# The chunk solve on off-diagonal 64x64 tiles, alternating with the next A K^T

## The chip, the cores and the metric

The kernel runs on one core of one Trainium2 chip. The metric is the device time of one execution in microseconds (us): 1723.08, the median of three runs from 1722.53 to 1729.99. Beside it stands one execution taken with the hardware profiler, 1721.11 us, whose traced span is 1719.3 us.

The engines go by the profile's names: PE is TensorE (PEld its weight load), DVE is VectorE, ACT is ScalarE, POOL is GpSimd, and SP is SyncE, which issues the DMAs. Every engine takes its own instructions in order.

## The reference

A two-layer encoder is applied to two groups of 512 tokens (width 1024, 16 heads of 64) with shared weights. Layer 0 is an RWKV-7 time mixing run forward and backward, layer 1 a neighbourhood attention on an 8 x 64 grid; a norm stands before and behind each. The part that matters here is the recurrence of layer 0, for each head and each direction:

```python
def step(s, inp):
    r_t, w_t, k_t, v_t, a_t, b_t = inp
    sa = jnp.einsum('bhvk,bhk->bhv', s, a_t)
    s = s * w_t[:, :, None, :] + sa[..., None] * b_t[:, :, None, :] + v_t[..., None] * k_t[:, :, None, :]
    return s, jnp.einsum('bhvk,bhk->bhv', s, r_t)
```

The kernel does it by chunks of 64 tokens. Within a chunk, the rows U that the term `sa` contributes solve a triangular system, whose right side Z takes the state before the chunk and a masked product A K^T times V. The inverse of the triangular matrix is made ahead. The norm that also plays a part is `x * rsqrt(mean(x*x) + eps) * g`.

## The kernel before

**Stages.** A prelude normalises both groups and does the first projections. `scan_phase` follows: the chunked recurrence of both groups, with the rest of the projections (`flow`) filling PE. `rest` does the attention and the output projections.

**The scan.** The work is a list of 8 items (group s, four heads pb), each with 8 chunks: 64 steps (`Step`, q = 0 to 63). A step holds both directions d, both pairs of heads g, and both heads h of a pair; on the 128 partitions lie two halves of 64. `e = [i % 2, 1 - i % 2]` says which half of the partitions the direction d uses in chunk i. In one step PE does, in this order:

- L1093, only if a chunk went before: the state times the chunk's factors, into the place `zy`, 32 records (a matmul in fp32 is two records in the trace).
- L1099: masked A K^T times V, added in `zy`, 16 records. ACT copies the result as Z (L1105).
- L1119, the solve: U = M Z, 8 matmuls with 64 rows, 64 columns and 64 moving columns, into `us`. Input and output lie in the same half (`r`), so they sit on the diagonal tiles of the 128x128 array, and d, the innermost loop, changes from the one to the other.
- `factors(q + 1)`: the next step's A K^T (L1010, 8 such matmuls on the diagonal tiles, into `room`, the free half of the first bank of this step's `zy`), and its 16 factor matmuls (L1022, into `pf`). If the next chunk isn't there yet, the thread `alone` does them later.
- L1133 and L1137: ACT has copied U into X (L1125), whose other half of the partitions is V, loaded by DMA in `fetch_x`. Tm times X gives the state's update, R times X the output.

DVE masks A K^T (L1045, `near`) and the factors (L1055, `outer`), and updates the state (L1145, L1146).

**What sets the order.** In the scan a planner writes the instructions of PE, DVE and ACT down in a fixed order. Each part of the work is a generator (`Thread`) that yields the engine it wants next, a gate, and the time at which its inputs are there. `weave` keeps a model of the engines' times (`Clock`) and picks the thread that is ready with the lowest rank: steps 0, `near` 0.5, `outer` 1, the norm of the first group 1.2, products (L747 to L749) 9. For PE the model has this rule, in `Clock.matmul`:

```python
for (r, q), x in self.tiles.items():
    if r == tp[0] or q != tp[1]:
        t = max(t, x)
self.tiles[tp] = t + c
self.t["P"] = t + (13.0 if f32 and not tr else 6.5)
```

So it lets a matmul begin beside another one only if that one has the same column half and other rows. `bank(tag)` returns a gate (is a place of this PSUM pool free in the model?) and a time (from when); most PE parts of the scan yield both.

**The norm.** `rstds` (L425) reduces the sum of squares with four matmuls of one column (L430), takes the root, and spreads the result with four matmuls (L442); each of the two takes a place in the pool `pm`. In the scan it runs twice, as part of the thread `norm0(0)`, and yields "P" without a gate. In `rest`, `norm0(1)` is put down together with the output projection of the first group: after each yield that projection goes on by 64/17 of its yields.

Of the kernel before, what the change touches and what calls it, by code (L numbers as in the profile page):

```python
# [2 lines left out]

# [1 line left out]

# [13 lines left out]
P = 128  # L19
# [5 lines left out]
L = 64  # L25
# [24 lines left out]
class Clock:  # L50
# [39 lines left out]
    def room(self, key, bufs):  # L90
        s = self.slots.get(key, ())
        return 0.0 if len(s) < bufs else min(self.left(n) for n in s)
# [121 lines left out]
class Trunk:  # L214
# [69 lines left out]
    def t(self, tag, shape=(P, T), bufs=1, dt=F32, pool=None):  # L284
        x = (pool or self.main).tile(list(shape), dt, tag=tag, bufs=bufs, name=self.name(tag))
        self.clock.new(x.tensor.name, (tag, id(pool or self.main)), bufs)
        return x
# [137 lines left out]
    def rstds(self, acc):  # L425

        nc = self.nc
        ps = self.p("pm", (P, 4))
        for c in range(4):
            nc.tensor.matmul(ps[:, c:c + 1], acc[:, c * P:(c + 1) * P], self.ones[:, 0:1], start=True, stop=True)  # L430
        yield "A"
        r = self.t("rs", (P, 4), 2)
        nc.scalar.activation(r, ps, AF.Sqrt, bias=self.eps[:, 0:1], scale=1.0 / D)
        yield "D"
        nc.vector.reciprocal(r, r)
        dg = self.tmp()
        for c in range(4):
            nc.vector.tensor_scalar(dg[:, c * P:(c + 1) * P], self.ident, r[:, c:c + 1], None, op0=ALU.mult)
        yield "P"
        out = self.p("pm")  # L440
        for c in range(4):
            nc.tensor.matmul(out[:, c * P:(c + 1) * P], self.ones, dg[:, c * P:(c + 1) * P], start=True, stop=True)  # L442
        yield "A"
        nc.scalar.copy(acc, out)
# [545 lines left out]
    def fetch_x(self, st):  # L990
        sp, s, pb, i, e = self.sp, st.s, st.pb, st.i, st.e
        half = lambda h: slice(64 * h, 64 * h + 64)

        st.X = self.t("X", (P, 2, 2, 2, HD), self.NX, F32, self.front)
        for d in range(2):
            self.load(
                st.X[half(1 - e[d]), d].rearrange("t h g c -> t h (g c)"),
                sp["vt", s][pb, i % 2, i // 2, :, :, d].rearrange("h t g c -> t h (g c)"))

    def factors(self, q):  # L1000


        nc, st = self.nc, self.steps[q]
        half = lambda h: slice(64 * h, 64 * h + 64)
        ab, e = st.ab, st.e
        st.ak = self.steps[q - 1].room if q else self.p("pm", (P, 2, 2, L))
        for g in range(2):
            for dd in range(2):
                for h in range(2):
                    nc.tensor.matmul(  # L1010
                        st.ak[half(h), dd, g], ab[half(h), dd, g, 1 + e[dd]], ab[half(h), dd, g, 2 - e[dd]], start=not q, stop=True,
                        skip_group_check=True)
        st.f = self.p("pf", (P, 2, T)).rearrange("p h (x d g t) -> p h x d g t", x=2, d=2, g=2)
        for d in range(2):
            for g in range(2):
                for a in range(2):
                    for h in range(2):
                        rt = ab[half(h), d, g, 3 - 3 * e[d]]

                        both = bass.AP(  # L1020
                            tensor=rt.tensor, offset=rt.offset, ap=[list(rt.ap[0]), [(16 - 8 * d - 4 * g - 3 + 3 * e[d]) * L, 2], [1, L]])
                        end = nc.tensor.matmul(  # L1022
                            st.f[half(a), h, 0, d, g] if st.last else st.f[half(a), h, :, d, g], ab[half(h), d, g, 2 * e[d] + a],
                            rt if st.last else both, start=True, stop=True)
        st.ends = [end]
        self.clock.keep.add(st.f.tensor.name)
        self.did["factors"] += 1
# [12 lines left out]
    def near(self, q):  # L1040

        nc, did, st = self.nc, self.did, self.steps[q]
        yield "D", lambda: did["factors"] > q, lambda c: c.at([st.ak.tensor.name])
        st.AK = self.t("AK", (P, 2, 2, L), self.NAK, F32, self.front)
        nc.vector.tensor_tensor(st.AK, st.ak, self.mstrict.unsqueeze(1).unsqueeze(1).broadcast_to([P, 2, 2, L]), op=ALU.mult)  # L1045
        did["AK"] += 1
# [20 lines left out]
    def step(self, q):  # L1067

        nc, did, st = self.nc, self.did, self.steps[q]
        vt, act = nc.vector, nc.scalar  # L1070
        t = lambda tag, shape, n: self.t(tag, shape, n, F32, self.front)
        half = lambda h: slice(64 * h, 64 * h + 64)
# [4 lines left out]
        free, room = self.bank("zy")  # L1077
# [6 lines left out]
        ab, e = st.ab, st.e  # L1084
# [3 lines left out]
        if st.i:  # L1088
            for d in range(2):
                for g in range(2):  # L1090
                    for a in range(2):
                        for h in range(2):
                            nc.tensor.matmul(  # L1093
                                zy[half(a), h, (a + e[d]) % 2, g], ab[half(h), d, g, 2 - 2 * e[d] + a], before.S[half(h), d, g],
                                start=(d == g == 0), stop=False, skip_group_check=True)
        for g in range(2):
            for d in range(2):
                for h in range(2):
                    nc.tensor.matmul(  # L1099
                        zy[half(e[d]), h, 0, g], st.AK[half(h), d, g], st.V[half(h), d, g],  # L1100
                        start=(st.i == g == 0), stop=True, skip_group_check=True)
        did["states"] += 1
        yield "A"
        Z = t("Z", (P, 2, 2, HD), self.NZ)
# [3 lines left out]
        go = lambda: q + 1 < len(self.steps) and did["factors"] == q + 1 and did["fetch"] > q + 1 and near()  # L1108
# [3 lines left out]
        mt = self.formed[key][1].rearrange("p (h i g) a t -> p h i g (a t)", h=2, i=NCH)  # L1112
        us = self.p("us", (P, 2, 4, HD))
        u = us[:, 0].rearrange("p (h g) v -> p h g v", h=2)
        for g in range(2):
            for h in range(2):
                for d in range(2):
                    r = half(e[d])
                    nc.tensor.matmul(u[r, h, g], mt[r, h, st.i, g], Z[r, h, g], start=True, stop=True)  # L1119
        did["solve"] += 1  # L1120
        if go():
            self.factors(q + 1)
        yield "A", lambda: did["X"] > q
        for d in range(2):
            act.copy(st.X[half(e[d]), d], u[half(e[d])])  # L1125
        yield (
            "P", lambda: did["R"] > q and did["X"] > q,
            lambda c: c.at(name(st.X, st.R[0], *([] if st.last else st.Tm[:1]))) - self.NEAR)
# [5 lines left out]
        for g, h in gh:  # L1134
            for d in range(2):
                r = half(1 - e[d])
# [418 lines left out]
    def scan_phase(self, mid):  # L1555
# [57 lines left out]
        def each(f):  # L1613
# [4 lines left out]
            Thread(lambda: 0, each(self.step)), Thread(lambda: 0.5, each(self.alone)), Thread(lambda: 0.5, each(self.near)),  # L1618
            Thread(lambda: 1, each(self.outer)),
            Thread(lambda: 0, fetch()), Thread(lambda: 0, fetch_x()), *self.flow(), Thread(lambda: 5, inverse()), Thread(lambda: 1.5, preps()),  # L1620
            Thread(lambda: 1.3 if did["finish"] == 3 else 4, finish()), Thread(lambda: 1.2, self.norm0(0))]
        e = mybir.EngineType
# [4 lines left out]
    def run(self):  # L1627
        self.todo = [(s, pb) for s in range(2) for pb in range(4)]
        self.made, self.hid, self.shift = set(), {}, {}
        self.did = Counter()  # L1630
        self.xz, self.os = [], [[], []]
        mid, prep, first = ExitStack(), ExitStack(), ExitStack()
        self.banks(mid, pf=1, pm=5 - self.SG - self.ZY, us=1)
        if self.SG:
            self.banks(mid, pg=self.SG)
        self.zs = ExitStack()
        self.banks(self.zs, zy=self.ZY)
        self.gt = "zy"
        self.lp = self.pool(first, "right")
        a = self.prelude(0)  # L1640
        for _ in range(self.FIRST):
            next(a)
        a = both(a, self.prelude(1))
        run(self.columns(0, "z", self.xz), (a, 1))
        run(self.columns(0, "k", self.shifted(0, 1)), (a, 1))
        run(a)
        self.xr = self.shifted(0, 0)
        first.close()
        self.front = self.pool(mid, "right")
        self.pp = self.pool(prep, "right")  # L1650
        self.AHEAD, self.AHEADW = self.SCAN_A, self.SCAN_W
        self.scan_phase(mid)
        self.rest(prep, mid)
# [58 lines left out]
def both(*gs):  # L1712
    for g in gs:
        yield from g
# [110 lines left out]
```

## Time and profile before

| What | us |
|---|---|
| median of three runs | 1723.08 |
| the profiled execution | 1721.11 |
| its span in the trace | 1719.3 |
| ahead of the scan | 0 to 280 |
| the scan, first A K^T to last chunk | 280 to 1149 |
| attention and output projections | 1149 to 1719 |

All times of the trace are microseconds from the start of the span. The span is 1.8 us shorter than the execution's own time. A row of the groups reads: line, engine, operation, output <- inputs, tile and shape, number of records, then busy time, mean length of one in ns, and the idle time of the engine before them with its releasers. The busy time of a group counts moments in which any of its records runs. The records of matmuls overlap (their ends are modelled), so the distance from one start to the next tells what one costs. A row of the table by stage gives, for each engine, the busy time and the number of its instructions, then the granted clock of PE as a share of full speed, the share of DMA and its GB/s. A row of the waits reads: who waited for whom, the sum in us, how often, the longest.

### The profile page before, as it was taken

What the parts mean: (1) busy time and instruction counts of PE and PEld (TensorE: products, weight loads), DVE (VectorE), ACT (ScalarE), POOL (GpSimd) and SP (SyncE); (2) the same over time, 40 slices, a digit from 0 to 9 for tenths busy, and PEclk for the clock granted to TensorE, in tenths of its full rate; (3) what the DMA queues carried; (4) which work ended last, traced back from release to release, by engine and by line L of the source; (5) the groups of instructions that cost most, each with busy time, mean ns of one, the idle gap of its engine ahead of it and who ended that gap; (6) DMA issues with size and microseconds to landing.
All of it is one profiled execution on the core that took longest, in us unless ns stands there. A gap on an engine that the chain in (4) does not pass through costs nothing. (4 is left out here: it accounts for less than half of the span.)

```text
span 1719.3 us, 45887 instructions
## 1 busy us (share of the span) xinstructions
PE 1583.5 (92%) x18624; PEld 1209.3 (70%) x18624; DVE 1246.5 (73%) x2725; ACT 982.9 (57%) x1975; POOL 24.1 (1%) x94
## 2 busy tenths in 40 slices
PE   7999787999988999789988799999999999999998
PEld 6766555776766767567766677777777787777776
DVE  8986678788877867898788898655565586555474
ACT  5444655767755675656576545544556664555462
POOL 0000000000000000000000000000000000000000
PEclk9989999999999989899999799999999999999999
DMA  5435687786566678766587564547564248555553
GB/s 204 166 117 202 208 278 230 221 273 224 184 201 205 206 239 252 240 217 216 188 263 229 191 209 146 177 147 246 178 197 146 93 147 268 163 164 160 163 169 98
DMA packets 240819, 336.23 MB, mean 196 GB/s; under 512 B 53696, under 2 KB 119360, under 8 KB 240608
## 3 DMA queue, kind: packets, MB, share of 16 engines
q1 hardware_dynamic: 240608, 333.31, 60.4%
q8 instruction: 146, 2.39, 0.6%
q14 instruction: 65, 0.53, 0.1%
HBM read 227.71 MB, written 105.51 MB: 194 GB/s over the span
## 5 line engine op out<-in xcount | busy, mean ns | idle before, releaser
L747 PE MATMUL pm<-act,whi 128*128 128x512 f32 x608 | 272.9, 449 | 13.1 <-ACT whi L699 9.9
L749 PE MATMUL pm<-act,wlo 128*128 128x512 f32 x608 | 248.8, 409 | 18.2 <-DVE wlo L701 18.2
L748 PE MATMUL pm<-act,whi 128*128 128x512 f32 x608 | 248.9, 409 | 7.7 <-DVE act L727 6.1
L404 PE MATMUL pg<-act,whi 128*128 128x512 f32 x448 | 181.4, 406 | 0.0
L405 PE MATMUL pg<-act,whi 128*128 128x512 f32 x448 | 178.1, 398 | 0.0
L406 PE MATMUL pg<-act,wlo 128*128 128x512 f32 x448 | 178.0, 398 | 0.0
L353 ACT CAST whi<-raw 128x512 fp32r<-128x512 f32 x156 | 96.2, 617 | 142.6 <-PE pg L405 71.8
L354 DVE TENSOR_TENSOR wlo<-raw,whi 128x512 fp32r<-128x512 f32 x156 | 106.7, 686 | 73.9 <-ACT whi L353 56.9
L747 PEld LDWEIGHTS pm<-act,whi 128*128 128x128 f32 x608 | 119.3, 196 | 56.3 <-issue 13.9
L749 PEld LDWEIGHTS pm<-act,wlo 128*128 128x128 f32 x608 | 119.9, 197 | 52.1 <-DVE wlo L701 25.4
L748 PEld LDWEIGHTS pm<-act,whi 128*128 128x128 f32 x608 | 120.1, 198 | 30.5 <-DVE act L727 8.6
L701 DVE TENSOR_TENSOR wlo<-raw,whi 128x512 fp32r<-128x512 f32 x152 | 102.8, 683 | 33.3 <-ACT whi L699 32.6
L699 ACT CAST whi<-raw 128x512 fp32r<-128x512 f32 x152 | 92.7, 617 | 27.9 <-PE pm L748 11.1
L404 PEld LDWEIGHTS pg<-act,whi 128*128 128x128 f32 x448 | 84.2, 188 | 23.7 <-issue 8.8
L406 PEld LDWEIGHTS pg<-act,wlo 128*128 128x128 f32 x448 | 84.2, 188 | 18.9 <-issue 2.8
L405 PEld LDWEIGHTS pg<-act,whi 128*128 128x128 f32 x448 | 84.3, 188 | 17.8 <-issue 3.0
L938 DVE TENSOR_TENSOR N<-etmp,N 128x30 f32<-128x30 f32 (+14 forms) x240 | 79.8, 332 | 8.3
L1361 DVE CUSTOM_DVE_ANT_0 sb<-pm,bias 128x256 f32<-128x256 f32 x128 | 50.1, 420 | 47.3 <-PE pm L1353 36.1
L937 DVE TENSOR_TENSOR etmp<-N 128x30 f32<-128x30 f32 (+14 forms) x240 | 78.7, 328 | 4.8
L1364 ACT ACTIVATE sb<-sb,mx 128x256 f32<-128x256 f32 x128 | 64.1, 502 | 30.7 <-DVE mx L1363 30.5
L1022 PE MATMUL pf<-cab 64*64 64x128 f32 (+1 forms) x2048 | 72.4, 270 | 3.4 <-issue 2.4
L1045 DVE TENSOR_TENSOR AK<-zy,cc 128x256 f32<-128x256 f32 x63 | 26.6, 422 | 64.2 <-PE zy L1010 64.0
(363 smaller groups left out, 3379.1 us busy)
## 6 DMA issues: line engine op xcount, KB each, us to landing
dab<-ab SPq DMA_DIRECT2D x32, 1024.0 KB, 7.1
cab<-dab SPq DMA_DIRECT2D x64, 512.0 KB, 4.5
raw<-in_w_in_dram SPq DMA_DIRECT2D x128, 256.0 KB, 2.9
bias<-in_rpb_dram SPq DMA_DIRECT2D x32, 384.0 KB, 4.7
raw<-in_w_z_dram SPq DMA_DIRECT2D x32, 256.0 KB, 4.6
dz<-tmp SPq DMA_DIRECT2D x32, 256.0 KB, 2.2
raw<-in_w_k_dram SPq DMA_DIRECT2D x32, 256.0 KB, 2.5
dk<-tmp SPq DMA_DIRECT2D x32, 256.0 KB, 3.0
```

The lines of the kernel that those rows point to most:

```text
L353: self.nc.scalar.copy(hi, src)
L354: (eng or self.nc.vector).tensor_tensor(lo, src, hi.bitcast(F32), op=ALU.subtract)
L404: nc.tensor.matmul(ps, hi, x[k][0], start=(k == 0), stop=False)
L405: nc.tensor.matmul(ps, hi, x[k][1], start=False, stop=False)
L406: nc.tensor.matmul(ps, lo, x[k][0], start=False, stop=(k == KT - 1))
L699: nc.scalar.copy(hi, raw[h])
L701: nc.vector.tensor_tensor(lo, raw.pop(h), hi.bitcast(F32), op=ALU.subtract)
L747: nc.tensor.matmul(ps, hi[:, at], xh, start=(k == 0), stop=False)
L748: nc.tensor.matmul(ps, hi[:, at], xl, start=False, stop=False)
L749: nc.tensor.matmul(ps, lo[:, at], xh, start=False, stop=(k == KT - 1))
L937: vt.tensor_tensor(tv, N[:, q + 1:, q:q + 1].broadcast_to([P, n, q]), N[:, q:q + 1, :q].broadcast_to([P, n, q]), op=ALU.mult)
L938: vt.tensor_tensor(N[:, q + 1:, :q], tv, N[:, q + 1:, :q], op=ALU.add)
```

## The change

1. The solve reads half r and writes U in the other half (off-diagonal tiles), r = 0, 1 innermost. X holds U and V in swapped halves, so `fetch_x`, the copy of U, and the output halves of the factors (`1 - a`) are swapped with it.
2. If the next step's factors are done together with the solve, the solve is handed to `factors` as a generator, and its matmuls alternate one by one with those of the next A K^T, whose heads now go in the order h = 1, 0.
3. `rstds` asks for a free place in `pm` ahead of each of its two PE parts, and has one more yield, at its start.

```diff
@@ rstds
         nc = self.nc
+        free, room = self.bank()
+        yield "P", free, room
         ps = self.p("pm", (P, 4))
...
-        yield "P"
+        yield "P", free, lambda c: max(room(c), c.at([dg.tensor.name]))
         out = self.p("pm")
@@ fetch_x
-                st.X[half(1 - e[d]), d].rearrange("t h g c -> t h (g c)"),
+                st.X[half(e[d]), d].rearrange("t h g c -> t h (g c)"),
@@ factors
-    def factors(self, q):
+    def pairs(self, q):
...
-                for h in range(2):
-                    nc.tensor.matmul(
+                for h in (1, 0):
+                    self.nc.tensor.matmul(
                         st.ak[half(h), dd, g], ab[half(h), dd, g, 1 + e[dd]], ab[half(h), dd, g, 2 - e[dd]], start=not q, stop=True,
                         skip_group_check=True)
+                    yield
+
+    def factors(self, q, beside=()):
...
+        for _ in zip_longest(beside, self.pairs(q)):
+            pass
...
-                            st.f[half(a), h, 0, d, g] if st.last else st.f[half(a), h, :, d, g], ab[half(h), d, g, 2 * e[d] + a],
+                            st.f[half(a), h, 0, d, g] if st.last else st.f[half(a), h, :, d, g], ab[half(h), d, g, 2 * e[d] + 1 - a],
@@ step
-        for g in range(2):
-            for h in range(2):
-                for d in range(2):
-                    r = half(e[d])
-                    nc.tensor.matmul(u[r, h, g], mt[r, h, st.i, g], Z[r, h, g], start=True, stop=True)
+
+        def solved():
+            for g in range(2):
+                for h in range(2):
+                    for r in range(2):
+                        nc.tensor.matmul(
+                            u[half(1 - r), h, g], mt[half(r), h, st.i, g], Z[half(r), h, g], start=True, stop=True)
+                        yield
+
+        both = go()
         did["solve"] += 1
-        if go():
-            self.factors(q + 1)
+        if both:
+            self.factors(q + 1, solved())
+        else:
+            run(solved())
         yield "A", lambda: did["X"] > q
         for d in range(2):
-            act.copy(st.X[half(e[d]), d], u[half(e[d])])
+            act.copy(st.X[half(1 - e[d]), d], u[half(1 - e[d])])
```

More of the change, by code (lines that the diff above doesn't have):

```diff
@@ L2 @@
 from contextlib import ExitStack, contextmanager
+from itertools import zip_longest
 import numpy as np
@@ L996, in fetch_x @@
             self.load(
-                st.X[half(1 - e[d]), d].rearrange("t h g c -> t h (g c)"),
+                st.X[half(e[d]), d].rearrange("t h g c -> t h (g c)"),
                 sp["vt", s][pb, i % 2, i // 2, :, :, d].rearrange("h t g c -> t h (g c)"))
-    def factors(self, q):
-        nc, st = self.nc, self.steps[q]
+    def pairs(self, q):
+        st = self.steps[q]
         half = lambda h: slice(64 * h, 64 * h + 64)
@@ L1008, in factors @@
             for dd in range(2):
-                for h in range(2):
-                    nc.tensor.matmul(
+                for h in (1, 0):
+                    self.nc.tensor.matmul(
                         st.ak[half(h), dd, g], ab[half(h), dd, g, 1 + e[dd]], ab[half(h), dd, g, 2 - e[dd]], start=not q, stop=True,
                         skip_group_check=True)
+                    yield
+    def factors(self, q, beside=()):
+        nc, st = self.nc, self.steps[q]
+        half = lambda h: slice(64 * h, 64 * h + 64)
+        ab, e = st.ab, st.e
+        for _ in zip_longest(beside, self.pairs(q)):
+            pass
         st.f = self.p("pf", (P, 2, T)).rearrange("p h (x d g t) -> p h x d g t", x=2, d=2, g=2)
```

## The prediction

> **What bounds the kernel now.** I read the page first, for the busy shares.
>
> ```profile
> span 1719.3 us, 45887 instructions
> PE 1583.5 (92%) x18624; PEld 1209.3 (70%) x18624; DVE 1246.5 (73%) x2725; ACT 982.9 (57%) x1975; POOL 24.1 (1%) x94
> ```
>
> TensorE (PE) is the busiest engine by far. The average says nothing of the stage that the change touches, so next came the table by stage: ahead of the scan, the scan (from the first A K^T to the last chunk), and the rest.
>
> ```profile
> core 0: us, PE busy (x) PEld busy (x) DVE busy (x) ACT busy (x) POOL busy (x), PEclk, DMA share, GB/s
> 0.00:280.00 280.00, 242.92 (x1389) 182.89 (x1389) 221.29 (x407) 151.73 (x276) 6.15 (x53) 0.95 0.59 196
> 280.00:1149.00 869.00, 783.38 (x14274) 596.32 (x14269) 686.21 (x1313) 524.10 (x1029) 18.00 (x41) 0.95 0.68 214
> 1149.00:1719.00 570.00, 557.17 (x2968) 430.07 (x2968) 339.01 (x1005) 307.07 (x670) 0.00 (x0) 1.00 0.52 167
> ```
>
> The scan takes 869 us, with PE busy 90% of it at a granted clock of 0.95, and VectorE (DVE) 79%. Its 64 steps come in bunches of eight, with stretches between in which the next chunk pair is prepared. One bunch, the stretch behind it, and the last two bunches in one:
>
> ```profile
> 640.00:698.00 58.00, 56.97 (x1335) 44.23 (x1334) 42.38 (x87) 34.59 (x76) 0.23 (x2) 1.00 0.77 229
> 698.00:786.00 88.00, 71.56 (x746) 52.81 (x744) 72.56 (x122) 55.99 (x104) 2.35 (x6) 0.86 0.74 240
> 1040.00:1149.00 109.00, 106.87 (x2552) 82.56 (x2552) 74.33 (x159) 48.29 (x102) 1.89 (x2) 1.00 0.51 161
> ```
>
> Inside a bunch PE is full (56.97 of 58, 106.87 of 109): between the matmuls of a step it does projection products, which fill what the step leaves. In the stretch behind the bunch PE has gaps, its clock falls to 0.86, and VectorE is as busy as PE. So a bunch is bound by PE, a stretch between bunches partly by VectorE.
>
> **What one step costs PE.** The timeline of one step (start, length, instruction, number of records; one fp32 matmul is two records) shows the changed part:
>
> ```profile
> 442.76 0.68 PE L1119 MATMUL us<-Z,MT 64*64 64x64 f32 x16
> 443.27 0.57 PE L1010 MATMUL zy<-cab 64*64 64x64 f32 x14
> 443.64 0.33 PE L1022 MATMUL pf<-cab 64*64 64x128 f32 x2
> 443.68 0.23 PE L1010 MATMUL zy<-cab 64*64 64x64 f32 x2
> 443.74 1.04 PE L1022 MATMUL pf<-cab 64*64 64x128 f32 x30
> ...
> 448.07 0.69 PE L1093 MATMUL zy<-S,cab 64*64 64x64 f32 x32
> 448.59 0.41 PE L1099 MATMUL zy<-V,AK 64*64 64x64 f32 x16
> 448.93 0.50 PE L747 MATMUL pm<-act,whi 128*128 128x512 f32 x1
> ```
>
> The solve (L1119, 16 records) holds PE from 442.76 to 443.27, 0.51 us. The next A K^T (L1010, 16 records) holds it from 443.27 to 443.74, 0.47 us. Together they take 0.98 us for 32 records. But L1093, 32 records of the same shape on the same 64x64 tiles, holds PE for only 0.52 us (448.07 to 448.59), half as long per record. The grouped rows say that this is so in all steps:
>
> ```profile
> L1119 PE MATMUL us<-Z,MT 64*64 64x64 f32 x1024 | 45.5, 230 | 1.8 <-ACT Z L1105 1.8
> L1010 PE MATMUL zy<-cab 64*64 64x64 f32 x1008 | 41.8, 224 | 0.9 <-DMA cab<-dab 0.9
> L1093 PE MATMUL zy<-S,cab 64*64 64x64 f32 x1792 | 39.8, 227 | 4.1 <-DVE y L1153 2.1 <-DVE S L1143 0.7 <-DVE S L1146 0.7
> L1099 PE MATMUL zy<-V,AK 64*64 64x64 f32 x1024 | 28.0, 224 | 7.9 <-issue 3.7 <-DVE etmp L937 3.6 <-DVE y L1153 0.6
> ```
>
> 45.5/1024 is 44 ns a record, 41.8/1008 is 41; 39.8/1792 is 22, 28.0/1024 is 27. The code tells the two sorts apart. L1119 and L1010 go back and forth between the two diagonal tiles (row half = column half) and write one PSUM bank. L1093 and L1099 send two neighbours in different row halves to one column half, and the two write different banks (the h halves of `zy`, 512 columns each). So two matmuls run side by side when the tiles share the columns and differ in rows and bank; on the diagonal they run one after the other. Which of the two conditions matters, this trace doesn't say.
>
> **The change, part by part.**
> 1. *The alternation.* The solve moves to tiles (0,1) and (1,0), and the A K^T, in the order h = 1, 0, follows each solve matmul. The tiles run (0,1), (1,1), (1,0), (0,0): each pair shares its columns, differs in rows, and writes two banks (the `us` place, and the room in `zy`). Both conditions of the fast rows hold. I take L1093's price: 32 records in 0.52 us instead of 0.98, so 0.46 less. Of the 64 solves about 61 are followed at once by the A K^T of the next step (two are followed by a product, one by a gap): 61 x 0.46 = 28 us of PE time in the scan. Bounds: nothing (the pairs don't overlap), and the same 32 records once more halved (0.26 us, if all four tiles ran together), 61 x 0.72 = 44 us.
> 2. *What it does to the chain.* The last solve matmul is issued some 0.5 us after the first, as now, so the copy of U into X starts when it did. The A K^T ends about 0.46 us sooner, and so do the factors behind it. The mask of A K^T on VectorE waits for just that:
>
> ```profile
> DVE AK L1045 <- PE zy L1010: 64.0, 42, 6.8
> ```
>    VectorE stands still 64.0 us in 42 such waits; 42 x 0.46 = 19 us of them can go. I don't add this, since PE binds in the bunches; it makes the gain of PE likelier to arrive.
> 3. *The added coupling.* The solve's later matmuls now stand behind the first A K^T, which needs the next chunk's `cab`. The row of L1010 above shows 0.9 us of waiting for that DMA, once. Cost 0 to 1 us; behind a late `cab` would stand the solve, the copy into X and the step.
> 4. *U and V swapped in X, a swapped in the factors.* Same instructions, same sizes, the other halves of the partitions: the loads of X, the copies (L1125) and the 16 factor matmuls keep number and shape. Cost 0.
> 5. *The norm's bunches.* In the scan the norm issues L430 and L442, twice each:
>
> ```profile
> 885.36 1.11 PE L430 MATMUL pm<-ones,acc 128*128 128x1 f32 x8 [1.16 <-DVE acc L1240]
> 887.76 1.91 PE L442 MATMUL pm<-tmp,ones 128*128 128x128 f32 x8
> ...
> 973.18 1.70 PE L430 MATMUL pm<-ones,vs 128*128 128x1 f32 x8
> 978.55 1.05 PE L442 MATMUL pm<-tmp,ones 128*128 128x128 f32 x8
> ```
>    The one wait (1.16) is for the accumulator, none is for a place, so asking for a place can gain about nothing. It can delay: a product column holds its place for 24 matmuls about 0.23 us apart (the last two rows of the next timeline below), 5.5 us, and the layer-1 operands stand behind the norm. One such delay costs PE nothing while other products are at hand. I take 0, with bounds of -1 and +6. In the last stage the two new yields let the first group's output run 2 x 64/17, some 7.5 steps, further while the second group's norm is put down. PE is busy 557.17 of 570 us there and VectorE 339.01; I take 0, bounds -2 and +2.
>
> **The sum.** 28 us of PE time are freed. PE was busy in 90% of the scan and nearly always in the bunches, but the stretches between them hang partly on VectorE, and the planner's order moves, since its own costs for these matmuls fall. I keep 85%: 24 us. From the profiled execution's 1721.11 us that is 1697; the median of the runs shown (1723.08) lies 2 us above that execution, so I say 1698.
>
> **Two rules of the Trainium skill that would give other numbers.** The page "TensorEngine Tiling (Array Packing)", section "Key Properties", says that different tiles can load weights and multiply in parallel. By it, four tiles in turn would run four at a time, and diagonal tiles side by side already; the trace disagrees, since L1119 takes 0.51 us for 16 records on two diagonal tiles, and L1093, which visits all four, gains a factor of two and not four. The page "TensorE: Matmul & The Clock Gate", section "Packing small matmuls — row/col tiling", says that a weight load overlaps running matmuls only where the row group differs. The new order has a neighbour in the same rows at each handover, (1,1) to (1,0) and (0,0) to (0,1), so by this rule the load would show there.
>
> **The rivals.**
> - *Four at a time.* If the four tiles did run together, a step would save 0.72 us: 44 us, 85% of it 37, 1684. Against it stands L1093. Chance 0.05.
> - *The weight load shows at each handover.* A step has 8 pairs, so 8 handovers within the same rows; L1093's order hands over from (1,0) to (0,1), other rows. The nearest price is a whole record on one tile, 0.51/16 = 0.032 us: 8 x 0.032 = 0.26 of the 0.46 would go. 61 x 0.20 x 0.85 = 10 us stay: 1711. Against it: in L1119 the two records of a matmul are on one tile, each with its own load, and still follow at 32 ns, so a load in the same rows seems hidden already. Chance 0.08.
> - *The change doesn't do what it says.* The pairs run one after the other for a reason that the trace doesn't show: 1721. Chance 0.07.
> - *PE time is freed but not used.* VectorE becomes the bound. In the scan it is busy 686.21 and stands 64.0 us before the mask alone, 750 of 869; in 698 to 786 it is busier than PE. Bunches get shorter, and the stretches between longer, for the inverse that the next bunch needs still has its VectorE work. A third of the 24 us would be left: 1713. Chance 0.15.
> - *Slower: PE starves more often.* This is the price of one starvation:
>
> ```profile
> 720.05 0.40 PE L748 MATMUL pm<-act,whi 128*128 128x512 f32 x1
> 724.43 0.80 PE L749 MATMUL pm<-act,wlo 128*128 128x512 f32 x1 [3.98 <-DVE wlo L701]
> 725.02 0.63 PE L747 MATMUL pm<-act,whi 128*128 128x512 f32 x1
> 725.45 0.63 PE L748 MATMUL pm<-act,whi 128*128 128x512 f32 x1
> ...
> 729.23 0.39 PE L749 MATMUL pm<-act,wlo 128*128 128x512 f32 x1
> 729.46 0.39 PE L747 MATMUL pm<-act,whi 128*128 128x512 f32 x1
> ```
>    PE waits 3.98 us for split weights; then matmuls start 0.43 us apart (725.02, 725.45), and from 729.23 on 0.23 apart again. In 4.8 us at about half speed 2.4 are lost, so some 6 us in all. A faster PE eats the stock of split weights sooner, and VectorE, which makes them, isn't faster. To be slower by over 0.5% the kernel would have to lose 24 + 8.6 = 33 us, so more than five such events beyond those of today, in seven stretches. Six give 1697 + 37 = 1734. For it: the scan loses 86 us to idle PE already. Against it: the last bunches are full. Chance 0.10.
>
> **How the numbers follow.** The forecast (pairwise overlap, most of it arrives) has the remaining 0.55, its own range 1687 to 1709 (all 28 us and a few of order to the good; half of it). 0.5% of the median is 8.6 us, about what a measurement of this kernel can tell from no change. Faster: the forecast 0.55, four at a time 0.05, of the weight load 0.05, of the unused time 0.07: 0.72. Within: the rest of these two, 0.03 and 0.08, and no overlap, 0.07: 0.18. Slower: 0.10. The range from 1682 to 1721 leaves out the slower case, half of no overlap and some of four at a time, 0.16 in all.
>
> **What would show it.** *Right:* the records of L1119 and of L1010 share one stretch, and the first factor matmul starts some 0.5 us after the first solve, not 0.98; the wait of L1045 shrinks well below 64.0; the last stage begins some 24 us earlier and keeps its 570 us. *Weight load or no overlap:* that stretch lasts about 0.75 or 0.98. *Unused:* the stretch is 0.5 long, but the scan is as long as now, with more idle PE in the stretches between bunches. *Slower:* more slices with a low granted clock, and more waits of L749 for `wlo`. The norm's part is wrong if the operands of the layer-1 group arrive late and PE waits for them behind L442.

## The result, and the profile after

The changed kernel takes 1715.49 us (median of 8 runs, 1708.78 to 1724.02), the kernel before 1726.64 (8 runs, 1722.53 to 1731.70). The ratio is 0.9937, with a 95% interval from 0.9917 to 0.9957: faster by 0.63%, some 11 us. That is more than the 0.5% that the prediction took as the bound, though the interval reaches down to 0.43%. The prediction had the sign right, and its 24 us were more than twice what came.

The page of the changed kernel, the same two lines as of before:

```profile
span 1712.3 us, 45893 instructions
PE 1561.7 (91%) x18624; PEld 1181.6 (69%) x18624; DVE 1245.2 (73%) x2725; ACT 988.0 (58%) x1979; POOL 24.1 (1%) x94
```

PE is busy 21.8 us less (1583.5 before) with the same 18624 records. The span is only 7.0 us shorter. So most of what PE saved stands on the page as more idle PE.

The alternation itself, from the timeline of the changed kernel (L1132 is now the solve, L1012 the A K^T, L1034 the factors):

```profile
325.83 0.27 PE L1132 MATMUL us<-Z,MT 64*64 64x64 f32 x1
325.84 0.27 PE L1012 MATMUL zy<-cab 64*64 64x64 f32 x1
325.84 0.27 PE L1132 MATMUL us<-Z,MT 64*64 64x64 f32 x1
325.85 0.27 PE L1012 MATMUL zy<-cab 64*64 64x64 f32 x1
...
326.30 0.22 PE L1132 MATMUL us<-Z,MT 64*64 64x64 f32 x1
326.31 0.22 PE L1012 MATMUL zy<-cab 64*64 64x64 f32 x1
326.35 1.05 PE L1034 MATMUL pf<-cab 64*64 64x128 f32 x32
```

From the first solve matmul (325.83) to the first factor matmul (326.35) are 0.52 us, where before there were 0.98. This is the value that the prediction took. The first four records, on the four tiles, start within 0.02 us.

The stages of the changed kernel (start and end, then for each engine the busy time, PE's clock, DMA):

```profile
0.00:280.00 280.00, 242.67 (x1369) 182.69 (x1373) 220.89 (x406) 151.92 (x276) 6.13 (x53) 0.95 0.59 195
280.00:1135.00 855.00, 752.63 (x14260) 561.68 (x14252) 682.25 (x1311) 526.33 (x1028) 18.00 (x41) 0.94 0.69 216
1135.00:1712.00 577.00, 566.36 (x3006) 437.21 (x3004) 342.02 (x1010) 309.72 (x675) 0.00 (x0) 0.99 0.52 167
```

The last chunk ends about 1135 instead of 1149, but then more of the projections is still to do: the last product of the scan's thread starts at 1171.4 against 1178.6, and from there both kernels need the same 541 us. In the scan PE's idle time rises from 86 us to 102 (855.00 less 752.63), though the scan is shorter.

The mask of A K^T on VectorE waits less:

```profile
DVE AK L1057 <- PE zy L1012: 29.3, 25, 4.7
```

Before it was 64.0 us in 42 waits.

### The profile page after: what moved, and what is told of

It is laid out like the page before. It is cut to its first block, busy times and chain, and to the rows that moved or that the text cites. A ratio compares the mean times of both kernels' runs of the same rounds, so it can differ in the third digit from the quotient of the medians.

```text
span 1712.3 us, 45893 instructions
## 1 busy us (share of the span) xinstructions
PE 1561.7 (91%) x18624; PEld 1181.6 (69%) x18624; DVE 1245.2 (73%) x2725; ACT 988.0 (58%) x1979; POOL 24.1 (1%) x94
## 5 line engine op out<-in xcount | busy, mean ns | idle before, releaser
L751 PE MATMUL pm<-act,whi 128*128 128x512 f32 x608 | 248.8, 409 | 11.8 <-DVE act L730 7.9
L702 ACT CAST whi<-raw 128x512 fp32r<-128x512 f32 x152 | 93.1, 618 | 32.4 <-PE pm L751 13.8
L1034 PE MATMUL pf<-cab 64*64 64x128 f32 (+1 forms) x2048 | 68.3, 271 | 2.9 <-issue 2.4
L1144 ACT COPY X<-us 64x256 f32<-64x256 f32 x128 | 46.8, 366 | 35.2 <-PE zy L1012 32.6
```

Of the source, the lines that this page charges most:

```text
L702: nc.scalar.copy(hi, raw[h])
L751: nc.tensor.matmul(ps, hi[:, at], xl, start=False, stop=False)
```

## Experiments

Two theories stood at the start, and a third was added after the first four runs. **A:** the freed PE time builds up a lead, which is given back at one place, the layer-1 operands, where PE waits for the norm. The two traces suggest it: the changed kernel is 14.1 us ahead at the first layer-1 column of products (900.5 against 914.6) and 0.6 behind at the third (983.4 against 982.8). **C:** the planner's new order, or the norm's waiting for places, costs what is missing. **V**, the third: VectorE is so near to being the bound that PE's freed time turns into waiting. It is the rival "PE time is freed but not used" of the prediction.

The planner writes its choices in one fixed order of threads. For several runs that order was written out and played back (3591 choices), so that the matmuls and the order could be changed one without the other. All times are medians, and each ratio is to the kernel before, run again beside the kernel in question (its medians there are 1724.36 to 1725.55).

### The norm's part alone

```diff
 # before.py, rstds
+        free, room = self.bank()
+        yield "P", free, room
         ps = self.p("pm", (P, 4))
...
-        yield "P"
+        yield "P", free, lambda c: max(room(c), c.at([dg.tensor.name]))
```

> Before, plus only the norm's two requests for a free place. Theory A (the alternation frees its 22 us of PE time, and the lead is given back at one place, the layer-1 operands, which PE doesn't set): the norm's part is worth nothing, ratio 0.997 to 1.003. Theory C (the norm's waiting for places eats the gain): slower by 5 to 12 us, ratio 1.003 to 1.007.

Measured: 1726.05 us against 1724.42, ratio 1.0004 (0.9983 to 1.0025). The norm's part is worth nothing that can be measured. C falls as far as it rests on the norm.

### The alternation in the old order

```diff
 # after.py, weave: the choices of the kernel before with the norm's part
-            best, wake = None, []
...
+        for c in PICKS:
+            t = threads["0123456789abcdefghijklmnop".index(c)]
+            ck.t["P"] = ck.pe()
+            t.step()
+            t.end = ck.note() or t.end
```

> The changed kernel, but the planner's choices are those that it makes for the kernel before with the norm's part: the matmuls of the solve alternate, everything else stands in the old order. Theory A: a gain of 5 to 12 us, as the change, for the place where the lead is lost is the same in both orders. Theory C (the new order is bad): a gain of 15 to 25 us, more than the change.

Measured: 1710.81 us against 1724.42, ratio 0.9916 (0.9889 to 0.9944). Against the norm's part alone, which has the same order, that is 15 us less. It lies between the two expectations and decides nothing by itself.

### The old matmuls in the new order

The same playback, with the choices of the changed kernel, in the kernel before with the norm's part.

> The kernel before with the norm's part, solve and A K^T one after the other on the diagonal, but with the planner's choices of the changed kernel. Theory A: no gain, ratio 0.998 to 1.004, and PE busy some 22 us longer than in the changed kernel. Theory C (the new order costs something): slower by 8 to 15 us, ratio 1.005 to 1.009. If the new order were what brought the gain, this would be 8 to 12 us faster than before.

Measured: 1727.70 us, ratio 1.0015 (0.9999 to 1.0030). The new order alone brings nothing and costs little; the rest of C falls. Its page is the right partner for the changed kernel, since only the alternation differs:

```profile
span 1726.4 us, 45886 instructions
PE 1589.9 (92%) x18624; PEld 1211.0 (70%) x18624; DVE 1245.3 (72%) x2725; ACT 989.1 (57%) x1979; POOL 24.2 (1%) x94
```

At the same order, PE is busy 28.2 us less in the changed kernel (1589.9 to 1561.7). In a second execution of the same program (the last run below) it is 21.6 us less (1568.3), so a single page gives this sum only to some 7 us; the prediction's 28 us follow from the 0.46 us of a step. The medians differ by 12.2 (1727.70 to 1715.49). So 43% of 28 us arrives; the intervals of the ratios leave room for about 25 to 65%. In the old order it is 15 of 28.

A falls here too. At the same order the changed kernel's lead at the A K^T V of each step is, in its two executions:

| step | 8 | 16 | 24 | 32 | 40 | 42 | 48 | 62 |
|---|---|---|---|---|---|---|---|---|
| us freed until then (0.46 a step) | 3.7 | 7.4 | 11.0 | 14.7 | 18.4 | 19.3 | 22.1 | 28.5 |
| us ahead | -1.0 | 0.6 | 1.7 | 6.1 | 12.1 | 12.3 | 11.6 | 11.6 |
| us ahead, second execution | 1.4 | 3.4 | 4.3 | 6.5 | 6.2 | 8.5 | 8.2 | 8.4 |

The layer-1 operands lie between steps 40 and 48, and no lead is lost there. The big lead and its loss, seen against the kernel before, belong to the new order, for the old matmuls in that order show them too (2.2 ahead at the first layer-1 column and 12.3 behind at the third). The lead fails to form instead. Of the 11 us freed in the first 24 steps 1.7 came, in the second execution 4.3; of the 10 us freed from step 40 to 62, none and 2.2. Two executions of one program differ by up to 6 us here (12.1 and 6.2 at step 40), so a single place is not to be read closely.

Three bunches, in each from its second step to its last, first of the old matmuls in the new order, then of the changed kernel:

```profile
330.61:383.16 52.55, 47.90 (x1095) 36.74 (x1089) 45.53 (x96) 33.40 (x73) 0.23 (x2) 1.00 0.83 254
665.81:710.88 45.07, 44.11 (x1084) 34.64 (x1079) 40.04 (x83) 31.23 (x69) 0.23 (x2) 1.00 0.77 227
1101.00:1143.16 42.16, 41.03 (x940) 31.14 (x935) 23.03 (x43) 17.63 (x37) 0.00 (x0) 1.00 0.60 187
```

```profile
330.73:383.46 52.73, 46.97 (x1094) 35.52 (x1089) 45.78 (x96) 33.05 (x73) 0.23 (x2) 0.97 0.84 259
663.01:708.94 45.93, 41.91 (x1085) 32.06 (x1080) 40.96 (x86) 32.19 (x70) 0.23 (x2) 1.00 0.79 236
1091.66:1131.06 39.40, 38.32 (x941) 28.44 (x936) 22.86 (x43) 17.58 (x37) 0.00 (x0) 1.00 0.61 200
```

A bunch frees six times 0.46, 2.8 us. In the last one VectorE is busy 23.03 of 42.16 us, 55%, and the bunch gets shorter by all of it, 2.76. In the first and the fourth VectorE is busy 87% and 89%, and here they get no shorter (+0.18 and +0.86). In the fourth PE's idle time grows instead, from 0.96 to 4.02 us. In the first PE is busy only 0.93 us less, at a granted clock of 0.97 in place of 1.00, so part of the gain seems to go to the clock there.

This fits theory V, but doesn't show it. In the second execution the fourth bunch is shorter by 1.04, and the third, with VectorE at 87% as well, loses 1.7 and 1.4. And in the fourth bunch of the changed kernel the waits of PE hardly name VectorE:

```profile
PE zy L1105 <- issue: 1.4, 1, 1.4
PE pf L898 <- issue: 1.1, 1, 1.1
PE zy L1156 <- issue: 0.7, 2, 0.5
PE us L1152 <- ACT X L1144: 0.3, 1, 0.3
PE zy L1105 <- DVE S L1165: 0.3, 1, 0.3
```

"issue" is idle time for which the profile shows no releaser: 3.2 of these 3.8 us. By what path PE is held there stays open. Whether VectorE's load is behind it is for the next two runs to tell.

### VectorE relieved, with and without the alternation

```diff
 # inverse: both kernels, in the order of the changed one
             yield "D"
+            if q > 1:
+                continue
             vt.tensor_tensor(tv, ..., op=ALU.mult)
             vt.tensor_tensor(N[:, q + 1:, :q], tv, N[:, q + 1:, :q], op=ALU.add)
```

> Leaves out 29 of the 30 rounds of the elimination on VectorE (464 of 480 instructions, some 155 us of its time), so that M isn't the inverse. Solve and A K^T one after the other on the diagonal, in the planner's order of the changed kernel. It is the base of the next one. All theories: faster than before by 20 to 120 us, since the stretches between the bunches hang on the elimination.

> The same with the solve alternating, in the same order; leaves out the same rounds. To be compared with the one before it. Theory V (VectorE's load holds the bunches, so PE's freed time becomes waiting): with VectorE relieved the 28 us arrive nearly whole, 20 to 28 us less than the one before it. Theory L (the step's own chain through PE, ACT and VectorE holds them, whatever else VectorE has to do): 8 to 14 us less, as with the elimination in place.

Measured: 1715.29 us (ratio to before 0.9946, 0.9928 to 0.9965) without the alternation, 1688.12 us (0.9790, 0.9773 to 0.9808) with it. The alternation brings 27.2 us here, nearly all of the 28. L falls, V stands.

The first of the two missed its own expectation: it is some 10 us faster than before, not 20 to 120. Against the same kernel with the elimination, the trace has the stretches between the bunches 16.0 us shorter in all, and the bunches as long as before (368.9 us in both). So the stretches hang on the elimination only for a small part.

The pages, first without, then with it:

```profile
span 1714.3 us, 45421 instructions
PE 1590.9 (93%) x18624; PEld 1210.2 (71%) x18624; DVE 1107.6 (65%) x2261; ACT 988.8 (58%) x1979; POOL 24.1 (1%) x94
```

```profile
span 1686.4 us, 45430 instructions
PE 1558.0 (92%) x18624; PEld 1181.1 (70%) x18624; DVE 1106.9 (66%) x2261; ACT 987.8 (59%) x1979; POOL 24.1 (1%) x94
```

The four kernels of one order make a table:

| median, us | elimination in place | left out (138 us of VectorE) |
|---|---|---|
| solve and A K^T one after the other | 1727.7 | 1715.3 |
| alternating | 1715.5 | 1688.1 |

Each relief alone brings 12 us, both together 40. The four were not run beside one another, but the ratios to before say the same: 0.7 and 0.8% alone, 2.25% together. One engine's work hides behind the other's here; neither is the bound by itself.

The bunches agree in part. With VectorE relieved, the first and the fourth bunch, which had gained nothing, and the second one are, without and then with the alternation:

```profile
324.02:375.88 51.86, 47.92 (x1095) 36.74 (x1090) 32.71 (x58) 33.38 (x73) 0.22 (x2) 1.00 0.93 287
432.38:480.50 48.12, 47.63 (x1081) 35.42 (x1076) 31.46 (x56) 32.85 (x71) 0.23 (x2) 1.00 0.70 218
657.08:704.40 47.32, 44.18 (x1083) 34.72 (x1079) 30.50 (x55) 31.56 (x70) 0.23 (x2) 1.00 0.80 247
```

```profile
324.32:373.56 49.24, 45.51 (x1095) 34.23 (x1090) 32.62 (x58) 32.95 (x73) 0.23 (x2) 1.00 0.88 270
430.50:478.72 48.22, 45.07 (x1079) 32.83 (x1075) 31.93 (x56) 32.99 (x71) 0.23 (x2) 1.00 0.70 221
650.43:695.62 45.19, 41.87 (x1085) 32.24 (x1080) 30.58 (x55) 32.03 (x70) 0.23 (x2) 1.00 0.83 254
```

The first is now shorter by 2.62, the fourth by 2.13. The second gains nothing (+0.10) even with VectorE at 65%. What holds that bunch stays open.

All eight bunches, and the time between them up to the last step, each as the change in us that the alternation makes:

| bunch | 1 | 2 | 3 | 4 | 5 | 6 | 7 | 8 | sum | between |
|---|---|---|---|---|---|---|---|---|---|---|
| VectorE busy without the alternation, % | 87 | 89 | 87 | 89 | 81 | 82 | 85 | 55 | | |
| elimination in place | +0.2 | +0.8 | -1.7 | +0.9 | -5.9 | -1.6 | -1.6 | -2.8 | -11.8 | -0.3 |
| the same, second execution | +0.1 | +1.2 | -1.4 | -1.0 | -1.5 | -1.3 | -1.0 | -2.8 | -7.8 | -1.0 |
| elimination left out | -2.6 | +0.1 | -2.3 | -2.1 | -4.0 | +0.2 | -2.2 | -2.8 | -15.7 | -7.5 |

So VectorE's load takes 4 to 8 us of the gain within the bunches, and some 7 us between them. It isn't a matter of the bunches alone, as theory V put it, and the busy share of a single bunch doesn't tell what that bunch will gain. The last 4.7 us of the 27.9 by which the two spans differ lie behind the scan, where neither kernel is changed; they have no explanation here.

### PE time added

```diff
 # before.py with the norm's part, in the new order
-                    nc.tensor.matmul(u[r, h, g], mt[r, h, st.i, g], Z[r, h, g], start=True, stop=True)
+                    for _ in range(2):
+                        nc.tensor.matmul(u[r, h, g], mt[r, h, st.i, g], Z[r, h, g], start=True, stop=True)
```

> The kernel before with the norm's part, in the planner's order of the changed kernel, and each solve matmul issued twice into the same place: 64 x 0.51 = 33 us more of PE, nothing else. Compared with old_code_new_order (1727.7). Theory V with PE and VectorE in balance (taking PE time away brings 43%, since VectorE is next; adding PE time must cost nearly all of it, since then PE is alone the bound): slower by 24 to 34 us. If PE time is worth 43% both ways: slower by 12 to 17 us.

Measured: 1754.95 us against 1724.36 before, ratio 1.0171 (1.0139 to 1.0204). Against the same kernel with one solve (1727.70) it is 27 us more, by the ratios too. The page:

```profile
span 1756.5 us, 47929 instructions
PE 1622.3 (92%) x19648; PEld 1244.4 (71%) x19648; DVE 1247.0 (71%) x2725; ACT 989.1 (56%) x1979; POOL 24.1 (1%) x94
```

PE is busy 32.4 us longer (1622.3 less 1589.9), and 27 of it, some 84%, is paid; of 28 us taken away 43% is gained. This fits two engines near balance. One rival is left: the doubled solve also ends some 0.5 us later in each step, and with it the copy into X, while the change left the end of the solve where it was. How much of the 27 us comes of that longer chain, this run doesn't tell.

### Which neighbours run side by side

The first of two runs keeps the solve on the diagonal and alternates it with the A K^T, so the neighbours of a pair lie in other rows, other columns and another bank. Both then use the same two tiles.

```diff
 # after.py
-                            u[half(1 - r), h, g], mt[half(r), h, st.i, g], Z[half(r), h, g], start=True, stop=True)
+                            u[half(r), h, g], mt[half(r), h, st.i, g], Z[half(r), h, g], start=True, stop=True)
```

(and U and V in X, and the factors' halves, back as before)

> The changed kernel, but the solve stays on the diagonal tiles and alternates with the A K^T on the other diagonal tile: neighbours differ in rows, columns and bank. If a shared column half is the condition for running side by side, the 32 records take 0.98 us as before, and the time is about that of before (ratio 0.997 to 1.003). If the two banks are the condition, they take 0.52 us, and the time is that of the change.

Measured: 1726.69 us, ratio 1.0009 (0.9992 to 1.0025). Its timeline:

```profile
330.36 0.27 PE L1132 MATMUL us<-Z,MT 64*64 64x64 f32 x1
330.37 0.27 PE L1012 MATMUL zy<-cab 64*64 64x64 f32 x1
330.47 0.22 PE L1132 MATMUL us<-Z,MT 64*64 64x64 f32 x1
330.48 0.27 PE L1012 MATMUL zy<-cab 64*64 64x64 f32 x2
330.53 0.22 PE L1132 MATMUL us<-Z,MT 64*64 64x64 f32 x1
330.59 0.22 PE L1012 MATMUL zy<-cab 64*64 64x64 f32 x1
330.59 0.27 PE L1132 MATMUL us<-Z,MT 64*64 64x64 f32 x2
...
331.29 0.22 PE L1132 MATMUL us<-Z,MT 64*64 64x64 f32 x1
331.34 1.04 PE L1034 MATMUL pf<-cab 64*64 64x128 f32 x30
```

From 330.36 to 331.34 are 0.98 us, as before the change. Two banks alone bring nothing.

It would be too quick to conclude that the neighbours must share the columns. The starts, which the trace holds to 1 ns, show that the two diagonal tiles do run side by side. A solve record and an A K^T record start 0.007 us apart (330.362 and 330.369), one on tile (0,0) and one on tile (1,1), and which of them is first changes as the code's order of the tiles does (330.527 for the A K^T, 330.534 for the solve). The next such pair follows 0.058 us later (0.107 after the first). The starts of L1119 and of L1010 in the kernel before lie in the same way: pairs 0.007 us apart, 0.058 us from pair to pair. In L1093 and in the changed kernel four records start within 0.02 us, and the next four again 0.058 us after.

So in all these kernels each tile starts a record every 0.058 us, beside the other tiles. The diagonal kept two tiles at work, the change keeps four. On two tiles each has 16 of the 32 records, 16 x 0.058 + 0.05 for the first = 0.98 us; on four each has 8, and 8 x 0.058 + 0.05 = 0.51.

The second run has the off-diagonal solve, but not the alternation:

```diff
 # after.py, factors
-        for _ in zip_longest(beside, self.pairs(q)):
-            pass
+        for _ in beside:
+            pass
+        for _ in self.pairs(q):
+            pass
```

> One part of the change alone: the solve on the two off-diagonal tiles and U and V swapped, but all its matmuls ahead of the A K^T, not alternating (with the norm's part). Neighbours within the solve and within the A K^T again differ in columns: the 32 records take 0.98 us, and the one time lies within 8 us of before. If the off-diagonal tiles alone were enough, 0.5 to 0.75 us.

Measured: one run, 1727.62 us, against 1724.36. In its timeline (L1134 is the solve, L1036 the factors):

```profile
325.23 0.51 PE L1134 MATMUL us<-Z,MT 64*64 64x64 f32 x10
325.52 0.27 PE L1012 MATMUL zy<-cab 64*64 64x64 f32 x2
325.57 0.28 PE L1134 MATMUL us<-Z,MT 64*64 64x64 f32 x3
...
325.69 0.22 PE L1134 MATMUL us<-Z,MT 64*64 64x64 f32 x1
...
326.04 1.04 PE L1036 MATMUL pf<-cab 64*64 64x128 f32 x30
```

The 32 records take 0.81 us, which neither expectation had. The A K^T goes to the two tiles that the solve leaves free, and it starts there at 325.52, while the solve goes on to 325.69. So the two overlap for a part; the alternation does the rest, since it has all four tiles at work from the start. Why the A K^T doesn't start earlier, and whether two tiles that share the columns also need two banks, no run shows.

### Two attempts to do better

The first gives PE more to do while the layer-1 operands are made:

```diff
 # after.py
-    NZ1, STOCK, EPS, NEAR = 6, 1, 60.0, 400.0
+    NZ1, STOCK, EPS, NEAR = 4, 1, 60.0, 400.0
```

> The changed kernel, with four product columns in place of two kept behind the output projection of the first group (NZ1 = 4), as work for PE while the layer-1 operands are made. If the lead is lost because PE has nothing to do there: faster than the change by 5 to 12 us. If it is lost in the bunches already: as the change, within 4 us.

Measured: 1721.19 us, ratio to before 0.9975 (0.9962 to 0.9987). It is worse than the change, by some 6 us, which neither expectation had. More cover at that place doesn't help, which agrees with the fall of A. Why it costs 6 us stays open; the planner's order moves with the setting.

The second relieves VectorE:

```diff
 # after.py, splits
-                nc.vector.tensor_tensor(lo, raw.pop(h), hi.bitcast(F32), op=ALU.subtract)
+                (nc.gpsimd if h % 3 == 1 else nc.vector).tensor_tensor(lo, raw.pop(h), hi.bitcast(F32), op=ALU.subtract)
```

> The changed kernel, with every third subtraction that splits the weights in the scan done by GpSimd in place of VectorE (some 27 us of VectorE's time in the scan). Theory V: faster than the change by up to 10 us. If GpSimd is too slow for it or disturbs VectorE: slower than the change.

Measured: 1750.89 us, ratio 1.0144 (1.0131 to 1.0157). The groups of GpSimd and of VectorE in the scan:

```profile
L704 POOL TENSOR_TENSOR wlo<-raw,whi 128x512 fp32r<-128x512 f32 x38 | 52.1, 1370 | 432.6 <-ACT whi L702 346.5 <-DVE act L732 27.8 <-PE pm L820 24.1
```

```profile
L704 DVE TENSOR_TENSOR wlo<-raw,whi 128x512 fp32r<-128x512 f32 x83 | 64.4, 776 | 37.0 <-ACT whi L702 33.5 <-DMA dab<-ab 2.4 <-DMA raw<-in_w_in_dram 0.9
```

One subtraction takes 1370 ns on GpSimd (spans of that engine are rough in the profile), and those left on VectorE take 776 ns in place of 685. So VectorE loses about 90 ns on each of the 83 and gives part of the relief back. PE's longest wait is now for `act` on ScalarE, 21.1 us in place of 4.0, and no wait of PE names GpSimd. By what path the 35 us against the changed kernel are lost stays open, and of theory V this run says nothing.

### The old order once more, beside the changed kernel

No edit: the alternation in the old order again, and the changed kernel with its own choices played back (the same program).

> The alternation in the old order once more, beside the changed kernel on one chip, to tell whether the old order makes the better version: ratio to before 0.990 to 0.994; within 4 us of the changed kernel if the two orders are worth the same, 4 to 8 us below it if the new order costs something.

> The changed kernel itself, its planner's choices written out (the same program), as the base of the one before: ratio to before 0.992 to 0.996.

Measured: 1709.34 us (ratio 0.9923, 0.9894 to 0.9952) and 1716.75 us (0.9951, 0.9933 to 0.9969). The old order lies 7.4 us below the new one here, which is what was expected if the new order costs something; the first runs of the two (1710.81 and 1715.49) were 4.7 apart. But the intervals overlap. It is the fastest full kernel measured here; that the old order is better is likely and not shown.

## Why the prediction was right or wrong

- **The fast pair (part 1): right in the number, wrong in the mechanism.** 0.52 us were taken and 0.52 came. PE's busy time at the same order fell by 28.2 us in one execution and by 21.6 in another, around the 28. But diagonal tiles don't run one after the other, as the prediction read from L1119: its 0.51 us are two tiles side by side, 8 records on each. L1093, which gave the price, is fast because it visits all four tiles, and the new order does too. That the price fitted is luck as far as the reading goes.
- **Which condition makes the pair fast: neither of the two that the prediction left open.** What counts is how many tiles are at work. The planner's rule in `Clock.matmul`, the same column half and other rows, is too narrow in the same way.
- **The rival "four at a time": its mechanism is what happens, its price is not.** Four tiles run at once already at 0.52 us; 0.26 would need a tile to take a record in half of 0.058 us. So the first of the two rules that the prediction set against its own reading, that different tiles work in parallel, agrees with the trace.
- **The weight load: not seen.** The page "TensorE: Matmul & The Clock Gate" of the Trainium skill, section "Packing small matmuls — row/col tiling", has a weight load overlap running matmuls only where the row group differs, and names the background weight buffer as another case. By the first alone the load would show at the handovers within the same rows. It doesn't: the 32 records need no longer than L1093's. What the buffer does, no run here shows.
- **The chain (part 2): right in direction.** The mask's wait fell from 64.0 to 29.3 us. At the same order it fell from 41.1 to 29.3 (30.8 in the second execution), 10 to 12 us, not 19; the rest came with the order.
- **The coupling to `cab` (part 3) and the swapped halves (part 4): right, the first within a few us.** PE waited 1.5 us at the A K^T for that DMA, and 3.8 in the second execution, instead of 0.9. That is little, if up to 3 us more in place of 1.
- **The norm (part 5): right.** It is worth nothing (1.0004), and the last stage keeps its 541 us.
- **"I keep 85%": wrong, and this is the step that failed.** 12.2 of 28 us arrived, 43%. It rested on the reading "a bunch is bound by PE", from PE's 56.97 of 58 us and 106.87 of 109. These are three of the eight bunches; from its second step to its last PE is busy only 37.71 of 46.77 us in the sixth, and 47.27 of 53.16 in the second. VectorE wasn't far behind PE either: it was busy 42.38 of the same 58 us, and it is 87 to 89% busy in the first four bunches of the new order. And a full PE shows only that a longer PE costs time, not that a shorter one gains it: plus 32 us of PE cost 27, minus 28 brought 12, and with 138 us of VectorE's work left out they brought 27. That VectorE's load decides is shown by this; how it holds PE up from step to step is not, since 5.8 of the 8.1 us of idle time that PE has more in the bunches come with no releaser in the profile.
- **The base: 3.6 us.** The prediction started from 1723.08; beside the changed kernel the kernel before took 1726.64. So 3.6 of the 17 us between 1698 and 1715.49 are not the change's.
- **The rival "PE time is freed but not used"** came nearest: VectorE as the next bound, with its 750 of 869 us counted out, and the time 1713. It got a chance of 0.15. Its place was wrong: it expected the bunches to shrink and the stretches between to grow. The bunches shrank by 8 to 12 of some 22 us, not at all in the first two, and the stretches between kept their sum.
- **Slower through starvation: no.** The old matmuls in the new order, which pays for such starvation if anything does, come out at 1.0015.

## What to carry to other kernels

Before crediting time taken from the busiest engine, read the second one in the same stage. Here PE was busy 90% of the scan and VectorE 79%: relieving PE alone paid less than half, loading it cost most of what was added, and only relieving both paid nearly in full. Test it by leaving out work of the second engine, since neither the busy shares of single bunches nor the waits told it. Read the starts of the records before naming a condition for their rate: 0.98 us looked like one tile after the other and was two tiles at a time. Trace a kernel twice before reading a difference of a few us at one place. When a planner rearranges everything, play its old choices back with the new code and its new choices with the old code; the comparison of the two traces alone pointed here to a place where nothing was lost.

## What the runs showed of the hardware

- fp32 matmuls on 64x64 tiles ran side by side on different tiles, also on the diagonal. Each tile started a record (64 moving columns) every 0.058 us: 32 records took 0.98 us on two tiles and 0.52 on four, in both orders of the four seen here, (0,0), (1,0), (0,1), (1,1) in L1093 and (0,1), (1,1), (1,0), (0,0) in the changed kernel.
- That every engine takes its instructions in order doesn't hold for the starts of PE's records on different tiles: with the off-diagonal solve in one block, the A K^T's first records start at 325.52 while solve records, issued earlier, start as late as 325.69, and the 32 records take 0.81 us.
- GpSimd needed 1370 ns, by its rough spans, for a subtraction of 128x512 that takes VectorE 685, and the mean of VectorE's own rose to 776 in that kernel.
